# A hybrid decoder block on one core: bias rows made early and copied inside DRAM, one product for the norm row, wider products for the mixer's transposed blocks

## Chip, core and metric

One core of a Trainium2 chip runs the whole program in one launch. The metric is the device time of one execution in microseconds. The kernel before has a median of 1972.65 us over three runs (1972.31 to 1973.14).

## What is computed

One layer over `x` of 256 rows by 2048 columns, all in float32:

```python
x = x + 0.5 * swiglu(rmsnorm(x, ffn1_norm), ffn1_w1, ffn1_w3, ffn1_w2)     # 2048 -> 5632 -> 2048
x = x + token_mix(rmsnorm(x, mix_norm), w_in, ...)
x = x + 0.5 * swiglu(rmsnorm(x, ffn2_norm), ffn2_w1, ffn2_w3, ffn2_w2)
return rmsnorm(x, final_norm)
```

`token_mix` projects `x` with one matrix `w_in` to the queries and keys of four retention heads, their values and gates, and the queries, keys and values of an attention of eight heads in two groups with three branches (compressed blocks, selected blocks, a window). The compressed branch runs 32 rows at a time through a small network (`cw1k`, `cw2k` for keys, `cw1v`, `cw2v` for values). A table of 8 heads by 32 buckets gives each logit a bias that depends on the distance of query and key alone; it is added in all three branches.

## The kernel before

**Products in two parts.** Every large weight comes as float32 tiles of 128 partitions by 1024 columns (512 KB). Class `Weights` takes them in one fixed order (`specs`): `load` starts a transfer on SP's queue into one of four `raw` buffers, `divide` makes `hi` by a cast on ScalarE (L153) and `lo` by a subtraction on VectorE (L154), three buffers of each. `next` gives the tile that is due and keeps two further tiles divided. The activations are split in the same way, and a product is three: hi by hi, lo by hi, hi by lo.

**Work between tiles.** `W.later(n, fn)` has `fn` written into the program when the n-th tile from now is taken; a scheduler then sets the order on each engine, and may place what depends on nothing far earlier. Each engine and each queue works in its order.

**Stages.** `ffn` runs twice: 176 tiles for the two upward matrices, in which a tile is 8 products of 512 columns and 8 of 256 (`up_tile`, L418 and L420: the moving operand of the first holds both parts of `x` side by side), then 88 tiles for the downward one (`unit_b`, L387 to L389). Between them lies `mixer`, with 152 tiles. Its results that are wanted transposed come from `pair_a`: two column blocks of 256 at a time, eight tiles, 24 products of 256 columns each (L366, L368, L370) into one accumulator a block; the caller reads the accumulators. There are eight such pairs: compressed keys and values; selected and window keys; two for the queries, the first with the tiles of `cw1k` and `cw1v` in turn with its own (`compress`, L683 to L685); four for the retention heads (`retain`, with `rotate`, `decay`, `values` laid between the next tiles). `attend` is laid between the tiles after the queries.

**Norms.** `norm_start` sums squares and makes `rs`, the reciprocal root, on POOL (L323, L324). `norm_row` turns it into a row that all partitions hold: two products of ones by a diagonal (`n1d`, one buffer, L339 and L340).

**The bias.** At the mixer's start SP's queue gets nine small loads (L568): `pe`, `relb` (the table), `oh` (97 rows of 2 KB that pick the bucket for each distance), `cs`, `cw2k`, `cw2v`, `cmask`, `dec`, `gn`. `bias_table` splits the table in three, makes one row a head (`vrow`, 8 by 384) with a product (L586), and writes it 128 times to DRAM from eight partitions (L592, `scr`, 1536 KB); six tiles later one load with a step of one element less a row reads it back as diagonals (L594, `bias`, 1024 KB).

Of the kernel before, what the change touches and what calls it, by code (L numbers as in the profile page):

```python
# [7 lines left out]
F32 = mybir.dt.float32  # L8
# [178 lines left out]
def body(tc, nc, I, out, keep, wp, st, pp, dr):  # L187
# [12 lines left out]
    def add(name, idx, n=1024):  # L200
        specs.append((I[name][idx], n))
# [22 lines left out]
    for k in range(3):
        add("win_a", 20 + k)
        add("cw1v", k)
    add("win_a", 19)
    add("cw1k", 3)
    add("win_a", 23)
    add("cw1v", 3)  # L230
    add_pair("win_a", 6, "win_a", 7)
# [6 lines left out]
    for h in range(RH):  # L238
        add_pair("win_a", 8 + 2 * h, "win_a", 9 + 2 * h)
# [115 lines left out]
    def pair_a(x, after=None):  # L355

        pa, pb = pm("pa"), pm("pb")
        for acc, c in [(pa, 0), (pa, 1), (pa, 2), (pb, 0), (pb, 1), (pb, 2), (pa, 3), (pb, 3)]:
            hi, lo = W.next()
            hi = hi[:, :1024].rearrange("p (k n) -> p k n", k=4)  # L360
            lo = lo[:, :1024].rearrange("p (k n) -> p k n", k=4)
            for f in range(2):
                o = acc[:, f * S:(f + 1) * S]
                cs = slice(f * P, (f + 1) * P)
                for k in range(4):
                    nc.tensor.matmul(o, lo[:, k, cs], x[c][:, k, 0, :], start=(c == 0 and k == 0 and f == 0),  # L366
                                     stop=False, skip_group_check=True)
                    nc.tensor.matmul(o, hi[:, k, cs], x[c][:, k, 0, :], start=False, stop=False,  # L368
                                     skip_group_check=True)
                    nc.tensor.matmul(o, hi[:, k, cs], x[c][:, k, 1, :], start=False,  # L370
                                     stop=(c == 3 and k == 3), skip_group_check=True)
            if after:
                after()
        return pa.rearrange("p (f s) -> p f s", f=2), pb.rearrange("p (f s) -> p f s", f=2)
# [125 lines left out]

    x2, x3 = [], []
# [5 lines left out]
    with tc.tile_pool(name="mx", bufs=1) as mp:  # L507
        mixer(nc, I, keep, mp, st, dr, ps, W, ident, x2, rs[1], lambda: norm_row(rs[1], "n1"),
              pair_a, unit_b, lhs_x(x2), rsqrt, into(x3, ss3, 2, 1.0))
# [35 lines left out]
    ffn(x3, lambda: norm_row(rs[2], "n2"), 5, finish, True)  # L545


def mixer(nc, I, keep, mp, st, dr, ps, W, ident, x2, rs, get_row, pair_a, unit_b, lhs, rsqrt, finish):
# [11 lines left out]
    oh = mp.tile([97, 2, 512], BF16, tag="L1", name="oh", bufs=2)  # L560
# [3 lines left out]
    relb = mp.tile([96, 8], F32, name="relb")  # L564
    w2 = [mp.tile([P, P], F32, name=f"w2{n}") for n in "kv"]
    for j, (t, n) in enumerate(((pe, "pe"), (relb, "relb"), (oh, "oh"), (cs, "cs"), (w2[0], "cw2k"), (w2[1], "cw2v"),
                                (cmask, "cmask"), (dec, "dec"), (gn, "gn"))):
        later(2 + j, lambda t=t, n=n: nc.sync.dma_start(t, I[n]))  # L568
# [52 lines left out]
    pc = pair_a(x2)  # L621
# [3 lines left out]
    kv = mp.tile([P, 2, G, S], F32, tag="t4", name="kv", bufs=3)  # L625
# [3 lines left out]
    def blocks(b):  # L629
        tt(kv[:, b], pc[b], row(R, 2), ALU.mult)  # L630
# [44 lines left out]
    turns = [(0, 0), (0, 1), (0, 2), (1, 0), (1, 1), (1, 2), (0, 3), (1, 3)]  # L675
# [13 lines left out]
    for j in range(2):  # L689
        for k, p in enumerate(pair_a(x2, compress if j == 0 else None)):  # L690
            h = 4 * j + 2 * k
            nc.vector.scalar_tensor_tensor(nq[:, h:h + 2, :], p, SCALE, row(R, 2), op0=ALU.mult, op1=ALU.mult)
# [109 lines left out]
    def retain(h, pq, pk):  # L802
        qk = mp.tile([P, 2, 2, S], F32, tag="t4", name="qk", bufs=3)

        def rotate(i, p):
# [34 lines left out]
        rotate(0, pq)  # L840
        later(1, lambda: rotate(1, pk))
# [3 lines left out]
    for h in range(RH):  # L845
        retain(h, *pair_a(x2))
# [60 lines left out]
```

## Time and profile before

| | |
|---|---|
| median of the runs | 1972.65 us |
| the profiled execution | 1973.32 us, its span 1971.5 us |
| TensorE busy | 1935.5 us (98%), weight loads 1677.7 us |
| VectorE, ScalarE, POOL busy | 1153.1, 893.6, 9.9 us |
| moved by DMA | 365.45 MB, mean 185 GB/s |
| granted clock of TensorE, mean | 0.993 |

Times in the rows are from the span's start. Products overlap: a row's duration is longer than the step to the next one, so pace is read from starts. The granted clock is a share of 2.4 GHz. DMA issues are not part of an engine's busy time; the issues of SP stand as SPq.

### The profile page before, as it was taken

To read this page: it belongs to the slowest core of one execution; us is meant where nothing else is said; L and a number is where in the kernel's file an instruction comes from. 1 tells how busy PE (TensorE), PEld (TensorE's weight loads), DVE (VectorE), ACT (ScalarE), POOL (GpSimd) and SP (SyncE) were. 2 spreads that over 40 slices of the span, in tenths; PEclk is the share of its full clock that TensorE was granted. 3 is DMA by queue.
4 is the path that set the end of the run, shared out by engine and by line. 5 is a ranking of instruction groups with operands and counts; after the bars stand their busy time and mean duration, and the time that the engine had idled before them with its cause. 6 is when DMAs were issued, how large, how long until landed. Compare 5 with 4: busy or idle time off the path is not lost.

```text
span 1971.5 us, 27203 instructions
## 1 busy us (share of the span) xinstructions
PE 1935.5 (98%) x10753; PEld 1677.7 (85%) x10753; DVE 1153.1 (58%) x1488; ACT 893.6 (45%) x1268; POOL 9.9 (1%) x27
## 2 busy tenths in 40 slices
PE   8999999999999999699999999999999999999998
PEld 7888888888888889598999888888888888888886
DVE  6666666666554446255677555666666666644444
ACT  6444444444444344244444444444444444434343
POOL 0000000000000000000000000000000000000000
PEclk9999999999999999799999999999999999999999
DMA  7666666666666656665444455666666666666664
GB/s 274 192 187 191 187 190 190 188 187 192 187 187 183 190 183 197 158 219 173 148 146 135 169 182 182 182 190 187 190 191 185 190 192 186 210 190 185 191 185 146
DMA packets 103354, 365.45 MB, mean 185 GB/s; under 512 B 11865, under 2 KB 14425, under 8 KB 102842
## 3 DMA queue, kind: packets, MB, share of 16 engines
q1 hardware_dynamic: 102794, 363.43, 60.3%
q8 instruction: 84, 1.38, 0.3%
q10 hardware_dynamic: 432, 0.29, 0.1%
q14 instruction: 44, 0.36, 0.0%
HBM read 360.00 MB, written 3.67 MB: 184 GB/s over the span
## 4 chain that ended last, share of the span: by engine, by line
PE 96%; DMA 3%; ACT 0%; DVE 0%; issue 0%; ACTq 0%; POOLq 0%; POOL 0%
PE pu L418 16%; PE pv L418 16%; PE p L388 12%; PE p L387 12%; PE p L389 12%; PE pu L420 8%; PE pv L420 8%; DMA raw<-in_cw1k 2%; PE pa L366 1%; PE pa L368 1%; PE pa L370 1%; PE pb L366 1%; PE pb L368 1%; PE pb L370 1%; PE up L418 1%; PE o L774 1%
## 5 line engine op out<-in xcount | busy, mean ns | idle before, releaser
L154 DVE TENSOR_TENSOR lo<-raw,hi 128x1024 fp32r<-128x1024 f32 (+2 forms) x673 | 823.9, 1224 | 649.1 <-ACT hi L153 648.6
L153 ACT CAST hi<-raw 128x1024 fp32r<-128x1024 f32 (+2 forms) x673 | 704.3, 1047 | 788.9 <-PE p L389 382.2
L387 PE MATMUL p<-hi,hh 128*128 128x512 f32 x704 | 279.4, 397 | 0.0
L388 PE MATMUL p<-lo,hh 128*128 128x512 f32 x704 | 278.7, 396 | 0.0
L389 PE MATMUL p<-hi,hl 128*128 128x512 f32 x704 | 278.6, 396 | 0.0
L418 PE MATMUL pu<-x3c,hi 128*128 128x512 f32 x672 | 264.5, 394 | 0.0
L418 PE MATMUL pv<-x1c,hi 128*128 128x512 f32 x672 | 264.3, 393 | 0.0
L418 PE MATMUL pu<-x1c,hi 128*128 128x512 f32 x672 | 264.3, 393 | 0.0
L418 PE MATMUL pv<-x3c,hi 128*128 128x512 f32 x672 | 264.3, 393 | 0.0
L420 PE MATMUL pu<-x1c,lo 128*128 128x256 f32 x672 | 189.5, 282 | 0.0
L420 PE MATMUL pu<-x3c,lo 128*128 128x256 f32 x672 | 189.2, 282 | 0.0
L420 PE MATMUL pv<-x1c,lo 128*128 128x256 f32 x672 | 189.2, 282 | 0.0
L420 PE MATMUL pv<-x3c,lo 128*128 128x256 f32 x672 | 189.1, 281 | 0.0
L389 PEld LDWEIGHTS p<-hi,hl 128*128 128x128 f32 x704 | 132.1, 188 | 32.3
L387 PEld LDWEIGHTS p<-hi,hh 128*128 128x128 f32 x704 | 132.5, 188 | 31.7
L388 PEld LDWEIGHTS p<-lo,hh 128*128 128x128 f32 x704 | 132.4, 188 | 31.1
L418 PEld LDWEIGHTS pu<-x3c,hi 128*128 128x128 f32 x672 | 126.2, 188 | 28.7 <-DVE u L195 0.2
L418 PEld LDWEIGHTS pu<-x1c,hi 128*128 128x128 f32 x672 | 126.3, 188 | 28.4 <-DVE u L195 0.2
L418 PEld LDWEIGHTS pv<-x3c,hi 128*128 128x128 f32 x672 | 126.2, 188 | 28.4
L418 PEld LDWEIGHTS pv<-x1c,hi 128*128 128x128 f32 x672 | 126.3, 188 | 28.3
L420 PEld LDWEIGHTS pv<-x3c,lo 128*128 128x128 f32 x672 | 126.7, 189 | 0.0
L420 PEld LDWEIGHTS pu<-x3c,lo 128*128 128x128 f32 x672 | 126.5, 188 | 0.0
(225 smaller groups left out, 2444.3 us busy)
## 6 DMA issues: line engine op xcount, KB each, us to landing
raw<-in_ffn_w SPq DMA_DIRECT2D x527, 512.0 KB, 3.7
raw<-in_win_a SPq DMA_DIRECT2D x64, 512.0 KB, 3.9
raw<-in_win_b SPq DMA_DIRECT2D x32, 512.0 KB, 3.2
raw<-in_wout SPq DMA_DIRECT2D x32, 512.0 KB, 3.3
raw<-in_win_vg SPq DMA_DIRECT2D x4, 560.0 KB, 3.8
xs<-in_x SPq DMA_DIRECT2D x2, 1024.0 KB, 9.7
raw<-in_cw1k SPq DMA_DIRECT2D x4, 512.0 KB, 21.6
raw<-in_cw1v SPq DMA_DIRECT2D x4, 512.0 KB, 4.5
```

The lines of the kernel that those rows point to most:

```text
L153: self.nc.scalar.copy(hi[:, s], raw[:, s])
L154: self.nc.vector.tensor_tensor(lo[:, s], raw[:, s], hi[:, s].bitcast(F32), op=ALU.subtract)
L366: nc.tensor.matmul(o, lo[:, k, cs], x[c][:, k, 0, :], start=(c == 0 and k == 0 and f == 0), stop=False, skip_group_check=True)
L368: nc.tensor.matmul(o, hi[:, k, cs], x[c][:, k, 0, :], start=False, stop=False, skip_group_check=True)
L370: nc.tensor.matmul(o, hi[:, k, cs], x[c][:, k, 1, :], start=False, stop=(c == 3 and k == 3), skip_group_check=True)
L387: nc.tensor.matmul(acc[t][:, :width], a, hi[:, k, :], start=first, stop=False)
L388: nc.tensor.matmul(acc[t][:, :width], a, lo[:, k, :], start=False, stop=False)
L389: nc.tensor.matmul(acc[t][:, :width], b, hi[:, k, :], start=False, stop=last)
L418: nc.tensor.matmul(acc, hi[:, k, f, :], xk.rearrange("p j s -> p (j s)"), start=(kt == 0), stop=False, skip_group_check=True)
L420: nc.tensor.matmul(acc[:, :S], lo[:, k, f, :], xk[:, 0, :], start=False, stop=(kt == KT - 1), skip_group_check=True)
L774: nc.tensor.matmul(o[:, q0:], v, p, start=start, stop=stop, skip_group_check=True)
```

## The change

- `relb` and `oh` are loaded at tile 40 of the first FFN and `vrow` is made at tile 60, both as written, in tiles that live through the whole program; POOL issues the transfers. `vrow` goes to DRAM once (`scr1`), and at tile 80 one transfer copies it 128 times from DRAM to DRAM (`scr`).
- The seven remaining small loads and the load of `bias` are issued by POOL at the mixer's start, and not by SP.
- `norm_start` makes both diagonals, and `norm_row` is one product of 256 columns.
- A block's tile is as in `up_tile`: 8 products of 512 columns and 8 of 256, into two accumulators. `close_a` adds their halves: a copy on ScalarE and an addition on VectorE for each accumulator, into SBUF, from where the callers read. The first pair keeps its order of tiles; all others are single blocks of four tiles (`block_a`), and the list of tiles follows. In the queries' first two blocks the four tiles of `cw1k` go with the first, those of `cw1v` with the second.

```diff
@@ tiles @@
-    for k in range(3):
-        add("win_a", 16 + k)
-        add("cw1k", k)
...
+    for j, n in enumerate("kv"):
+        for t in range(4):
+            add("win_a", 16 + 4 * j + t)
+            add(f"cw1{n}", t)
...
@@ norm_start, norm_row @@
-        return rs
-
-    def norm_row(rs, name):
+        dg = st.tile([P, 2, P], F32, tag="xg", name=name + "d", bufs=3)
+        for t in range(2):
+            nc.vector.tensor_scalar(dg[:, t, :], ident, rs[:, t:t + 1], None, op0=ALU.mult)
+        return rs, dg
+
+    def norm_row(dg, name):
         pr = ps(name + "p")
-        for t in range(2):
-            dg = st.tile([P, P], F32, tag="dg", name=name + "d", bufs=1)
-            nc.vector.tensor_scalar(dg, ident, rs[:, t:t + 1], None, op0=ALU.mult)
-            nc.tensor.matmul(pr[:, t * P:(t + 1) * P], ones, dg, start=True, stop=True)
+        nc.tensor.matmul(pr[:, :S], ones, dg.rearrange("p t s -> p (t s)"), start=True, stop=True)
@@ blocks @@
+    def tile_a(x, accs, c):
+        hi, lo = (w[:, :1024].rearrange("p (k n) -> p k n", k=4) for w in W.next())
+        for k in range(4):
+            xk = x[c][:, k]
+            for f, acc in enumerate(accs):
+                cs = slice(f * P, (f + 1) * P)
+                nc.tensor.matmul(acc, hi[:, k, cs], xk.rearrange("p j s -> p (j s)"), start=(c == 0 and k == 0),
+                                 stop=False, skip_group_check=True)
+                nc.tensor.matmul(acc[:, :S], lo[:, k, cs], xk[:, 0, :], start=False, stop=(c == 3 and k == 3),
+                                 skip_group_check=True)
+
+    def close_a(accs, dst):
+        for f, acc in enumerate(accs):
+            nc.scalar.copy(dst[:, f, :], acc[:, S:])
+            tt(dst[:, f, :], acc[:, :S], dst[:, f, :], ALU.add)
+
+    def block_a(x, dst, after=None):
+        accs = pm("pa"), pm("pa")
+        for c in range(CH):
+            tile_a(x, accs, c)
+            if after:
+                after()
+        close_a(accs, dst)
...
@@ bias, ahead of the first FFN @@
+    def bias_rows():
...
+        nc.gpsimd.dma_start(scr1, vrow[:, :384])
+
+    def bias_loads():
+        nc.gpsimd.dma_start(relb, I["relb"])
+        nc.gpsimd.dma_start(oh, I["oh"])
+
+    W.later(40, bias_loads)
+    W.later(60, bias_rows)
+    W.later(80, lambda: nc.gpsimd.dma_start(scr, bass.AP(tensor=scr1.tensor, offset=scr1.offset,
+                                                         ap=[[0, P], [384, 8], [1, 384]])))
@@ mixer @@
-        later(2 + j, lambda t=t, n=n: nc.sync.dma_start(t, I[n]))
+    for t, n in ((pe, "pe"), (cs, "cs"), (w2[0], "cw2k"), (w2[1], "cw2v"), (cmask, "cmask"), (dec, "dec"), (gn, "gn")):
+        nc.gpsimd.dma_start(t, I[n])
...
+    diag = bass.AP(tensor=scr.tensor, offset=scr.offset + 127, ap=[[8 * 384 - 1, P], [384, 8], [1, S]])
+    nc.gpsimd.dma_start(bias[:, :, 16:], diag)
...
-        later(2, lambda: nc.sync.dma_start(scr.rearrange("q h r -> h q r"),
-                                           vrow[:, None, :].to_broadcast([8, P, 384])))
-        later(8, lambda: nc.sync.dma_start(bias[:, :, 16:], diag))
...
@@ retain @@
-        rotate(0, pq)
-        later(1, lambda: rotate(1, pk))
+        block_a(x2, qk[:, 0])
+        rotate(0)
+        block_a(x2, qk[:, 1])
+        later(1, lambda: rotate(1))
```

**POOL, from the program's start to the mixer's, before** (`masks.py` makes the identity, `n0s` and `n1s` are the norms' reciprocal roots, L614 to L616 clear tiles of the mixer):

```order
masks.py:197 MEMSET ident 128x128
masks.py:199 ISA
masks.py:199 AFFINE_SELECT ident<-ident 128x128 [waits Pool_49]
L323 TENSOR_SCALAR n0s<-n0t 128x2 [waits DVE_49]
L324 TENSOR_TENSOR n0s<-n0s,mhalf 128x2 [waits Pool_49]
L614 MEMSET vcmp 128x256 [waits DMAHW3_49,DMAHW4_49,DMAHW2_49,DMAHW5_49,DMAHW0_49,DMAHW6_49,DVE_49,PE_49]
L615 MEMSET ptc 128x512
L616 MEMSET kcat 128x2
L323 TENSOR_SCALAR n1s<-n1t 128x2 [waits DVE_49]
L324 TENSOR_TENSOR n1s<-n1s,mhalf 128x2 [waits Pool_49]
```

The same stretch of the change:

```order
L535 DMA relb<-in_relb 96x8
masks.py:199 ISA
masks.py:199 AFFINE_SELECT ident<-ident 128x128 [waits Pool_49]
L536 DMA oh<-in_oh 97x1024
L320 TENSOR_SCALAR n0s<-n0t 128x2 [waits DVE_49]
L321 TENSOR_TENSOR n0s<-n0s,mhalf 128x2 [waits Pool_49]
L532 DMA scr_99<-vrow 8x384 [waits DVE_49]
L540 DMA scr<-scr_99 128x3072 [waits DMASW2_49]
L607 DMA pe<-in_pe 128x64 [waits DMAHW3_49,DMAHW4_49,DMAHW2_49,DMAHW5_49,DMAHW0_49,DMAHW6_49,DVE_49,PE_49]
L607 DMA cs<-in_cs 128x512
L607 DMA w2k<-in_cw2k 128x128
L607 DMA w2v<-in_cw2v 128x128
L607 DMA cmask<-in_cmask 128x16 [waits DMASW0_49]
L320 TENSOR_SCALAR n1s<-n1t 128x2 [waits DVE_49]
L607 DMA dec<-in_dec 128x1024 [waits DMASW1_49]
L321 TENSOR_TENSOR n1s<-n1s,mhalf 128x2 [waits Pool_49]
```

`relb` and `oh` stand at the very start and wait for nothing; `scr_99` is `scr1`. Five of the mixer's loads now stand ahead of `n1s`, and a sixth between its two steps.

**VectorE at the program's start, before** (`lo` is a weight's subtraction, `x1c` the first FFN's activations):

```order
L286 MEMSET mhalf 128x16
L154 TENSOR_TENSOR lo<-raw,hi 128x512 [waits DMAHW1_49,Activation_49]
L283 SCALAR_TENSOR_TENSOR x1c_74<-landed,gains,x1c_74 128x256 [waits DMAHW4_49,DMAHW0_49,Activation_49]
L283 SCALAR_TENSOR_TENSOR x1c_74<-landed,gains,x1c_74 128x256 [waits DMAHW2_49,Activation_49]
L154 TENSOR_TENSOR lo<-raw,hi 128x512 [waits DMAHW3_49,Activation_49]
```

And with the change:

```order
L523 CAST part_1722<-relb 96x8 [waits DMASW0_49]
L524 COPY rb<-part_1722 32x8 [waits DVE_49]
L195 TENSOR_TENSOR relb<-relb,part_1722 96x8
L523 CAST part_1723<-relb 96x8 [waits DVE_49]
L524 COPY rb<-part_1723 32x8 [waits DVE_49]
L195 TENSOR_TENSOR relb<-relb,part_1723 96x8
L523 CAST part_1724<-relb 96x8 [waits DVE_49]
L524 COPY rb<-part_1724 32x8 [waits DVE_49]
L154 TENSOR_TENSOR lo<-raw,hi 128x512 [waits DMAHW1_49,Activation_49]
L280 SCALAR_TENSOR_TENSOR x1c_74<-landed,gains,x1c_74 128x256 [waits DMAHW4_49,DMAHW0_49,Activation_49]
```

The table's eight operations, the first of which waits for the load that POOL issues, now stand ahead of the first subtraction.

**VectorE at the mixer's start, with the change** (`n1t` is the sum of squares, `xg` and `x2c` the last transposed activations):

```order
L326 TENSOR_REDUCE n1t<-ss_101 128x2 [waits Activation_49]
L594 TENSOR_TENSOR blk<-pe,blk 128x16x2 [waits DMASW4_49,Activation_49]
L594 TENSOR_TENSOR blk<-pe,blk 128x16x2 [waits Activation_49]
L154 TENSOR_TENSOR lo<-raw,hi 128x1024 [waits DVE_49,DMAHW0_49,PE_49,Activation_49]
L331 TENSOR_SCALAR n1d<-ident,n1s 128x128 [waits Pool_49]
L331 TENSOR_SCALAR n1d<-ident,n1s 128x128
L256 TENSOR_TENSOR xg<-pt,gains 128x512 [waits PE_49]
L154 TENSOR_TENSOR lo<-raw,hi 128x1024 [waits DMAHW1_49,DVE_49,Activation_49]
L195 TENSOR_TENSOR x2c_6433<-xg,x2c_6433 128x4x128 [waits Activation_49]
```

Both halves of `n1d` stand together and ahead of the next subtraction; before, the second one stood four subtractions later. `blk<-pe` has moved ahead of a subtraction.

## Rows read from the trace of the kernel before

**Rows 1.** Waits of TensorE over the whole span: line, whose work it waited for, us in total, times, longest.

```profile
PE phk L683 <- ACT hi L153: 18.8, 1, 18.8
PE up L418 <- DVE x1c L283: 3.0, 1, 3.0
PE n1p L340 <- DVE n1d L339: 1.6, 1, 1.6
PE up L418 <- ACT hi L153: 1.4, 1, 1.4
PE phk L684 <- DVE lo L154: 0.8, 1, 0.8
```

**Rows 2.** TensorE in order of time around its longest wait: start, duration, line, operation, and in brackets the idle time before it and what ended it.

```profile
805.70 0.28 PE L370 MATMUL pa<-x2c,hi 128*128 128x256 f32 x1
824.76 0.43 PE L683 MATMUL phk<-hi,blk 128*34 128x256 f32 x1 [18.79 <-ACT hi L153]
...
830.72 0.28 PE L370 MATMUL pa<-x2c,hi 128*128 128x256 f32 x1
```

**Rows 3.** Stretches: length, busy us and instructions of TensorE, its weight loads, VectorE, ScalarE, POOL; then granted clock, mean busy share of the DMA engines, GB/s.

```profile
172.00:228.00 56.00, 56.00 (x323) 49.25 (x322) 35.78 (x46) 26.95 (x41) 0.00 (x0) 1.00 0.63 188
...
794.00:797.00 3.00, 3.00 (x27) 3.00 (x26) 1.28 (x2) 1.05 (x1) 0.00 (x0) 1.00 0.46 49
...
827.00:830.00 3.00, 3.00 (x16) 2.79 (x15) 1.75 (x3) 1.25 (x2) 0.00 (x0) 0.50 0.76 221
...
833.00:836.00 3.00, 3.00 (x28) 2.97 (x26) 2.28 (x2) 1.56 (x2) 0.00 (x0) 1.00 1.06 402
...
1000.00:1030.00 30.00, 30.00 (x236) 29.33 (x235) 23.39 (x56) 12.63 (x28) 0.88 (x2) 1.00 0.42 126
```

**Rows 4.** SP's queue in order of time: start, duration of the issues, line, transfer, count.

```profile
754.92 0.33 SPq L568 DMA_DIRECT2D oh<-in_oh  x1
...
766.29 0.33 SPq L568 DMA_DIRECT2D dec<-in_dec  x1
...
788.53 0.31 SPq L592 DMA_DIRECT2D scr<-vrow  x1
790.42 9.37 SPq L140 DMA_DIRECT2D raw<-in_cw1k  x1
```

**Rows 5.** The chain that ended last, in order of time: start, us, what.

```profile
755.43 12.11 DMA raw<-in_win_a
...
790.42 33.14 DMA raw<-in_cw1k
```

**Rows 6.** DMA issues by line: transfer, issuer, count, KB each, median us from issue to landing.

```profile
raw<-in_ffn_w SPq DMA_DIRECT2D x527, 512.0 KB, 3.7
...
bias<-scr SPq DMA_DIRECT2D x1, 1024.0 KB, 7.0
...
relb<-in_relb SPq DMA_DIRECT2D x1, 3.0 KB, 2.8
```

**Rows 7.** In order of time, columns as in rows 2: SP issuing the load into a raw buffer just freed (this row merges six loads, the first at its start), ScalarE casting that tile, then TensorE at the first and the last product of two tiles of a block, and at the same product of two tiles of the first FFN, six tiles apart.

```profile
738.62 14.33 SPq L140 DMA_DIRECT2D raw<-in_win_a  x6
...
747.49 1.05 ACT L153 CAST hi<-raw 128x1024 fp32r<-128x1024 f32 x1 [1.75 <-PE p L389]
...
752.89 0.28 PE L366 MATMUL pa<-x2c,lo 128*128 128x256 f32 x1
...
758.48 0.28 PE L370 MATMUL pa<-x2c,hi 128*128 128x256 f32 x1
...
199.91 0.39 PE L418 MATMUL pu<-x1c,hi 128*128 128x512 f32 x1
...
216.64 0.39 PE L418 MATMUL pu<-x1c,hi 128*128 128x512 f32 x1
```

**Rows 8.** Groups of instructions by shape, the FFN's closing of two accumulators: line, engine, operation, count, busy us, mean ns, idle time before.

```profile
L439 ACT COPY r<-pu 128x256 f32<-128x256 f32 x84 | 31.3, 372 | 122.3 <-PE pu L420 122.3
L195 DVE TENSOR_TENSOR u<-pv,r 128x256 f32<-128x256 f32 x84 | 35.1, 418 | 0.0
```

**Rows 9.** The program's start: one stretch with the columns of rows 3, then VectorE and ScalarE in order of time.

```profile
10.00:15.00 5.00, 5.00 (x26) 4.27 (x26) 4.73 (x8) 4.39 (x9) 0.00 (x0) 0.85 1.05 413
...
7.71 0.88 DVE L283 SCALAR_TENSOR_TENSOR x1c<-landed,gains,x1c 128x256 fp32r<-128x256 f32 x2 [2.23 <-ACT x1c L282]
...
19.40 0.63 ACT L319 ACTIVATE junk<-xs 128x512 f32<-128x512 f32 x1 [1.02 <-DMA xs<-in_x]
```

**Rows 10.** Waits of SP's queue over the whole span: whose work, us, times, longest.

```profile
SPq L568 <- DMA oh<-in_oh: 4.2, 1, 4.2
```

**Rows 11.** The mixer's start in order of time: SP, POOL, VectorE, ScalarE.

```profile
753.08 1.32 SPq L568 DMA_DIRECT2D pe<-in_pe  x1
...
756.08 0.70 POOL L324 TENSOR_TENSOR n1s<-n1s,mhalf 128x2 f32<-128x2 f32 x1
...
756.82 0.29 DVE L339 TENSOR_SCALAR n1d<-ident,n1s 128x128 f32<-128x128 f32 x1 [1.10 <-POOL n1s L324]
...
758.80 1.05 ACT L153 CAST hi<-raw 128x1024 fp32r<-128x1024 f32 x1 [1.36 <-PE pa L370]
...
759.92 0.69 DVE L259 TENSOR_TENSOR xg<-pt,gains 128x512 f32<-128x512 f32 x1
760.52 1.22 DVE L154 TENSOR_TENSOR lo<-raw,hi 128x1024 fp32r<-128x1024 f32 x1
```

More of the change, by code (lines that the diff above doesn't have):

```diff
@@ L218, in body @@
     add_pair("win_a", 0, "win_a", 1)
-    add_pair("win_a", 2, "win_a", 3)
-    for k in range(3):
-        add("win_a", 16 + k)
-        add("cw1k", k)
[L224 to L231, printed above, removed]
+    for t in range(8, 16):
+        add("win_a", t)
+    for j, n in enumerate("kv"):
+        for t in range(4):
+            add("win_a", 16 + 4 * j + t)
+            add(f"cw1{n}", t)
+    for t in range(24, 32):
+        add("win_a", t)
     for t in range(4):
@@ L238, in body @@
     for h in range(RH):
-        add_pair("win_a", 8 + 2 * h, "win_a", 9 + 2 * h)
+        for t in range(8):
+            add("win_a", 32 + 8 * h + t)
     for t in range(16, 32):
@@ L372, in pair_a @@
+    def close_a(accs, dst):
[6 more added lines that the diff above has]
+            tile_a(x, accs, c)
             if after:
                 after()
-        return pa.rearrange("p (f s) -> p f s", f=2), pb.rearrange("p (f s) -> p f s", f=2)
+        close_a(accs, dst)
+    def pair_a(x, da, db):
+        aa, ab = [(pm("pa"), pm("pa")) for _ in range(2)]
+        for accs, c in [(aa, 0), (aa, 1), (aa, 2), (ab, 0), (ab, 1), (ab, 2), (aa, 3), (ab, 3)]:
+            tile_a(x, accs, c)
+        close_a(aa, da)
+        close_a(ab, db)
@@ L499, in into @@
         return f
+    oh = keep.tile([97, 2, 512], BF16, name="oh")
+    relb = keep.tile([96, 8], F32, name="relb")
+    rb = keep.tile([97, 8], BF16, name="rb")
+    scr1 = dr.tile([8, 384], F32, name="scr1")
+    scr = dr.tile([P, 8, 384], F32, name="scr")
+    def bias_rows():
+        part = [keep.tile([96, 8], BF16, name=f"part{j}") for j in range(3)]
+        for j in range(3):
+            nc.vector.tensor_copy(part[j], relb)
+            nc.vector.tensor_copy(rb[32 * j:32 * j + 32, :], part[j][32 * j:32 * j + 32, :])
+            if j < 2:
+                tt(relb, relb, part[j], ALU.subtract)
+        nc.vector.memset(rb[96:97, :], 1.0)
+        vp = ps("vp")
+        nc.tensor.matmul(vp[:8, :], rb, oh[:, 1, :], start=True, stop=True)
+        vrow = st.tile([8, 512], F32, tag="junk", name="vrow", bufs=1)
+        nc.vector.tensor_copy(vrow[:, :384], vp[:8, :384])
+        nc.gpsimd.dma_start(scr1, vrow[:, :384])
[6 more added lines that the diff above has]
+                                                         ap=[[0, P], [384, 8], [1, 384]])))
     x2, x3 = [], []
@@ L507, in body @@
     with tc.tile_pool(name="mx", bufs=1) as mp:
-        mixer(nc, I, keep, mp, st, dr, ps, W, ident, x2, rs[1], lambda: norm_row(rs[1], "n1"),
-              pair_a, unit_b, lhs_x(x2), rsqrt, into(x3, ss3, 2, 1.0))
+        mixer(nc, I, keep, mp, st, scr, oh, rb, ps, W, ident, x2, rs[1][0], lambda: norm_row(rs[1][1], "n1"),
+              pair_a, block_a, unit_b, lhs_x(x2), rsqrt, into(x3, ss3, 2, 1.0))
     ss4 = st.tile([P, 2, CH + 1], F32, name="ss4")
@@ L543, in finish, with mixer @@
                 nc.sync.dma_start(out[t * P:(t + 1) * P, 512 * k:512 * k + 512], x)
-    ffn(x3, lambda: norm_row(rs[2], "n2"), 5, finish, True)
-def mixer(nc, I, keep, mp, st, dr, ps, W, ident, x2, rs, get_row, pair_a, unit_b, lhs, rsqrt, finish):
+    ffn(x3, lambda: norm_row(rs[2][1], "n2"), 5, finish, True)
+def mixer(nc, I, keep, mp, st, scr, oh, rb, ps, W, ident, x2, rs, get_row, pair_a, block_a, unit_b, lhs, rsqrt, finish):
     later = W.later
@@ L638, in mixer @@
     later(4, lambda: tt(cs, cs, row(R, 2), ALU.mult))
-    pks, pkw = pair_a(x2)
-    tt(kcat[:, :, 16:], pks, row(R, 2), ALU.mult)
-    tt(kw, pkw, row(R, 2), ALU.mult)
+    for dst in (kcat[:, :, 16:], kw):
+        block_a(x2, dst)
+        tt(dst, dst, row(R, 2), ALU.mult)
     hidT = [mp.tile([P, 30], F32, name=f"hidT{b}") for b in range(2)]
@@ L674, in mixer @@
     ph = [ps("phk"), ps("phv")]
-    turns = [(0, 0), (0, 1), (0, 2), (1, 0), (1, 1), (1, 2), (0, 3), (1, 3)]
+    turns = [(b, i) for b in range(2) for i in range(4)]
     def compress():
@@ L687, in compress @@
             compress_end(b, ph[b])
[L689 to L692, printed above, removed]
+    for j in range(4):
+        q = nq[:, 2 * j:2 * j + 2, :]
+        block_a(x2, q, compress if j < 2 else None)
+        nc.vector.scalar_tensor_tensor(q, q, SCALE, row(R, 2), op0=ALU.mult, op1=ALU.mult)
     for j, width in ((0, 280), (1, 256)):
```

49 lines of the change are left out of this document (8 added, 41 removed).

## The prediction

> **What bounds the kernel now.** I read the waits of TensorE first [rows 1]. They show the reader that TensorE stands still for some 26 us of 1971.5, and that one wait makes most of it: 18.8 us before the first product of `compress` (L683), for the cast of a weight tile on ScalarE. The sequence of TensorE around it [rows 2] shows where it lies and that it costs more than its idle time: the last product before it starts at 805.70, the next at 824.76, another pause of 0.8 us follows for the subtraction [rows 1], and products go on slowly until 830.72. The stretches [rows 3] show why: after the pause, in 827 to 830, TensorE is busy throughout but the granted clock is 0.50 (1.2 GHz); in 833 to 836 it is 1.00 (2.4 GHz), and 28 products start in 3 us instead of 16.
>
> What the cast waits for stands in the queue of SP and in the chain [rows 4, 5]: at 788.53 SP issues `scr<-vrow` (1.5 MB), right behind it the load of a `cw1k` tile, which takes 33.14 us to land where a weight tile usually takes 3.7 [rows 6]. In 794 to 797 the sixteen engines move 49 GB/s, though their mean busy share is 0.46 [rows 3]: few of them work, and slowly. The weights are queued behind them on the same queue. So the bound is TensorE everywhere but here, at the first products, and at `n1p` (1.6 us) [rows 1].
>
> **How much lateness the weights bear.** It decides most of what follows. At 738.62 a raw buffer is free and SP loads into it; the cast of that tile starts at 747.49, waiting for a product and not for the load, which at the usual 3.7 us landed at 742.3, 5.2 us early. Cast and subtraction (1.05 and 1.22 us, [rows 7, 11]) end at 749.8, and with three `hi` buffers the products start two tiles after the cast began, at 753.1: another 3.3 us [rows 6, 7]. A transfer may thus come some 8.5 us late before TensorE waits. The trace agrees: behind `oh` a weight tile took 12.11 us, 8.4 more than usual [rows 5], and no product waited for it.
>
> **The change, part by part.**
>
> *The broadcast write leaves the mixer.* SP's queue no longer holds `scr<-vrow`, `oh`, or the other small loads. Gone is the whole delay of [rows 2]: without it, the product after 805.70 starts at 805.82, and 23 products (12 of `phk`, 11 of `pa`) at 0.117 to 0.119 us bring TensorE to 808.53; in the trace the next one starts at 830.72. That is **22.2 us**, clock included. The last weights before this stage came in time, and the stage's demand (tiles of 2.8 and 1.4 us in turn, so 512 KB in 2.1 us, 250 GB/s) is below the 402 GB/s that the queue reached in 833 to 836 [rows 3].
>
> *The norm row.* In the trace the second `n1d` waits for the first product (one buffer) and so falls behind a late subtraction; TensorE waits 1.6 us [rows 1]. Now both halves are made at once by `norm_start`, long before the product: **1.6 us** gone. One 256-wide product in place of two 128-wide ones changes under 0.2 us at three places; I put nothing down.
>
> *The transposed blocks.* A tile is now 8 products of 512 columns and 8 of 256, in place of 24 of 256. The old form: 48 products from 752.89 to the one that would follow 758.48 (758.60), so 2.855 us a tile. The new form is that of the FFN's `up_tile`: six tiles from 199.91 to 216.64, 2.788 us a tile [rows 7]. Eight pairs of blocks are 64 tiles: 64 x 0.067 = **4.3 us**. The columns are the same; what shrinks is the number of weight loads, 24 to 16.
>
> The price is `close_a`: for each of 16 blocks two copies on ScalarE and two additions on VectorE, by the FFN's rows 0.37 and 0.42 us [rows 8], so 0.74 and 0.84 us a block, in 11 us and more of products. VectorE is busy 0.78 of the fullest stretch (1000 to 1030) [rows 3]; 1.7 us more for a pair makes it 0.84. I cost it at nothing. The tightest place is the first pair, which takes all four accumulators: the next block wants the second accumulator of the first one about 3.1 us after its last product, and one cast, one subtraction and both closes (1.05 + 1.23 + 0.8) stand before it. If that cover is gone it costs tenths of a us, once. Products read `qk` three tiles after its block ends, as before, with some 3 us more work ahead of them in 8.4 us.
>
> *The early loads.* The order shows that `relb` and `oh` are issued by POOL at the program's very start, not at tile 40, and that VectorE has the splitting of `relb` ahead of its first subtraction. Here the sixteen engines are full: 413 GB/s in 10 to 15 us [rows 9]. 197 KB more at that rate are 0.5 us, and they come out in full, since TensorE waits for casts behind `xs`, the last of these loads [rows 1, 9]. `relb` took 2.8 us on SP [rows 6]; issued at about 1 us, with 1.3 us for the eight small operations, it is done before the first `x1c` at 7.71. From below the cost is 0. From above it is the trace's own `oh`: issued at 754.92, and SP, which waited 4.2 us for its landing, goes on at 766.29 [rows 4, 10]: 11.4 us for 194 KB, what one engine of sixteen would need and not sixteen. I take **+0.5**, nearer to the lower end, since this queue is another one, and keep 11.4 for the range.
>
> *The copy inside DRAM*, 1.5 MB early in the first FFN, beside weights at 188 GB/s [rows 3] of 400 or so. On free engines it takes 1.5 MB / 210 GB/s = 7.5 us; at the pace of `scr<-vrow` itself, 33 us. With half of the engines' time the weights keep 200 GB/s, so nothing is lost in the first case; in the second they lose at most a quarter of their pace for 33 us, 8 us, about their slack. Nothing put down. The loads at the mixer's start, 2 MB with `bias<-scr` (which landed in 7.0 us beside weights [rows 6]), are covered in the same way.
>
> *POOL's queue.* `n1s` now stands behind five DMA issues, and a sixth between its two steps. VectorE has `n1d` in order behind it, and behind that the subtraction of a tile cast at 758.80, whose products start 5.9 us later, at 764.7. 0.6 + 0.7 + 1.2 us of VectorE lie between, so `n1s` may come at 762.2; before it was ready at 756.8 [rows 7, 11]. No row has a DMA issue of POOL. The unhindered ones of SP are 0.33 to 1.32 us [rows 4, 11]: six are 2 to 7.9 us from 753.1, and `n1s` at 756 to 762, just in time. I take **+0.5** for the wait on `pe` and on this, 0 and 5 as ends.
>
> The sum goes against the profiled execution, 1973.3 us (span 1971.5): 1973.3 - 22.2 - 1.6 - 4.3 + 0.5 + 0.5 = **1946.2 us**. The median of the runs, 1972.65, lies 0.7 lower, well inside the range.
>
> **Rivals.**
>
> *`oh` on one engine at the start.* For it: the 11.4 us of [rows 4, 10]. Against it: the new queue, of which no row tells. That engine would share its time between `oh` and its part of every first load; `xs` would land some 8 us later, and TensorE pays it: **1954 us** (1951 to 1957). The Trainium skill ("DMA: Bandwidth & Descriptors", section "Why a DMA increments its semaphore by 16 and not by 1") says that the number of engines is the largest divisor up to 16 of the slowest dimension, so 1 for 97 rows, and 8 for the 8 rows of `vrow`; by that rule the sum would be this rival's 1954 us. The trace agrees on the queue of SP. The same section says that some copies issued by POOL are spread by rows over up to 16 engines all the same, which no run here shows.
>
> *POOL too slow for `n1s`.* If an issue takes 2 us or more, `n1s` comes at 766 or later and VectorE's queue, the weights' subtractions in it, stands: 3 to 6 us, **1950 us**. The Trainium skill ("SBUF — State Buffer", section "SBUF: two separate sides") says that VectorE in some modes keeps POOL from writing descriptors, which would do this; no row here shows it.
>
> *The copy or the gather takes more of the weights' time than their slack.* The wait moves rather than goes: half of it back, **1957 to 1965 us**. For it: such transfers were slow here. Against it: the weights are no longer behind them in one queue.
>
> *Slower.* The copy of 1.5 MB runs on one engine in the first FFN. By the pace of `oh` it takes 92 us alone; an engine that the weights need for 0.63 of the time gives them half while it lasts, some 185 us, and every tile waits for its slowest part: 185 x (1 - 0.5/0.63) = 38 us, less 8.5 of slack. It decides from 28 + 8.5 us of lost weight time; with long pieces of the copy taking more than half, it is more: **1975 to 2000 us**. Against it: the copy has 128 rows, and `bias<-scr`, with as many, moved 1 MB in 7.0 us [rows 6].
>
> **How the numbers follow.** Forecast (1943 to 1949): 0.62. `oh` narrow: 0.14. POOL late: 0.13. Transfers over the slack: 0.06. Slower or back to nothing: 0.03. Better than 1943: 0.02. The range takes in the first three: 1941 to 1957. A measurement here tells about 0.2%, 4 us, from no change. Faster by more than that are all cases but the last rival and the tail of the fourth: 0.95; within it 0.02, slower 0.03.
>
> **What would show it.** Right: no wait of TensorE at the first `phk` product; granted clock 1.00 throughout 800 to 840; about 2.79 us a tile in the blocks; weights landing in some 4 us around `scr<-scr1`. Wrong: a longer first 30 us (`oh`), VectorE idle before `n1d` or before `blk<-pe` at the mixer's start (POOL), casts that wait for DMA during the copy or the gather, or waits of TensorE for the closes.

## The result and the profile after

The changed kernel takes **1948.33 us** (median of 4 runs, 1948.16 to 1949.17), beside 1972.89 for the kernel before in the same session: ratio 0.9873, 95% interval 0.9862 to 0.9885, so 24.6 us less. The forecast was 1946.2 in a range of 1941 to 1957. The time lies in the range, 2.1 us over the forecast. The profiled execution took 1949.17 us (span 1947.4), 0.84 over the median, against 1973.32 (1971.5) before: 24.15 us less.

TensorE's waits of 0.5 us and over, which answer to [rows 1] (columns as there):

```profile
PE up L429 <- DVE x1c L280: 4.1, 1, 4.1
PE up L429 <- ACT hi L153: 1.8, 1, 1.8
PE warm L286 <- DVE ones L282: 1.0, 1, 1.0
PE up L431 <- DVE lo L154: 0.5, 1, 0.5
```

The waits at `phk` and at `n1p` are gone. All that is left lies in the first 30 us, and there it has grown: 4.1 us where [rows 1] has 3.0.

Four stretches with the columns of [rows 3]: part of the start, the copy inside DRAM, the place of the old wait, the 30 us in which VectorE is fullest.

```profile
5.00:10.00 5.00, 0.87 (x5) 0.58 (x4) 2.64 (x11) 1.28 (x3) 0.00 (x0) 1.00 0.96 314
...
186.00:197.00 11.00, 11.00 (x65) 9.67 (x64) 6.49 (x9) 5.37 (x8) 0.54 (x1) 1.00 0.91 287
...
800.00:840.00 40.00, 40.00 (x264) 35.37 (x262) 26.87 (x33) 20.94 (x26) 0.00 (x0) 1.00 0.74 227
...
1030.00:1060.00 30.00, 30.00 (x173) 26.28 (x173) 24.98 (x54) 13.73 (x28) 0.88 (x2) 1.00 0.49 151
```

In 800 to 840 TensorE is busy throughout at a granted clock of 1.00; before, [rows 2, 3] had 19 us of idle time there and then 0.50. The copy takes place beside full work of TensorE. VectorE, with the closes, is busy 0.83 of its fullest 30 us; before, the fullest was 0.78 [rows 3], at an earlier time, since the mixer's work has moved.

The start in order of time, which answers to [rows 9]: POOL's two loads, then who waits for what.

```profile
1.28 0.73 POOL L535 DMA_DIRECT2D relb<-in_relb  x1 [0.36 <-issue]
2.37 0.60 POOL L536 DMA_DIRECT2D oh<-in_oh  x1
6.79 0.17 DVE L523 CAST part<-relb 96x8 bf16<-96x8 f32 x1 [5.68 <-DMA relb<-in_relb]
8.72 0.91 ACT L279 ACTIVATE x1c<-landed,gains 128x256 fp32r<-128x256 f32 x2 [3.93 <-DMA gains<-in_gains]
...
21.68 0.63 ACT L316 ACTIVATE junk<-xs 128x512 f32<-128x512 f32 x1 [1.39 <-DMA xs<-in_x]
```

And the issues, time to landing last, which answer to [rows 6]:

```profile
scr<-scr POOLq DMA_DIRECT2D x1, 1536.0 KB, 9.9
bias<-scr POOLq DMA_DIRECT2D x1, 1024.0 KB, 10.5
...
oh<-in_oh POOLq DMA_DIRECT2D x1, 194.0 KB, 7.6
...
gains<-in_gains ACTq DMA_DIRECT2D x1, 24.0 KB, 7.0
relb<-in_relb POOLq DMA_DIRECT2D x1, 3.0 KB, 5.5
```

`gains` (24 KB) lands 7.0 us after its issue; in the trace of before it was 5.4. The first `x1c` waits for it, and `xs` then comes 2.3 us later: `junk<-xs` starts at 21.68, in [rows 9] at 19.40. From 5 to 10 us the DMA engines move 314 GB/s, and 397 before, at nearly the same busy share (0.96 and 1.03). The trace of before, columns of [rows 3]:

```profile
5.00:10.00 5.00, 2.00 (x8) 1.61 (x7) 2.50 (x5) 2.83 (x6) 0.00 (x0) 0.81 1.03 397
```

The mixer's start, which answers to [rows 11]: POOL issues before and between the two steps of `n1s`.

```profile
756.55 0.58 POOL L607 DMA_DIRECT2D pe<-in_pe  x1 [569.40 <-DVE xs L499]
...
759.32 0.19 POOL L320 TENSOR_SCALAR n1s<-n1t 128x2 f32<-128x2 f32 x1
759.57 0.58 POOL L607 DMA_DIRECT2D dec<-in_dec  x1
...
760.17 0.74 POOL L321 TENSOR_TENSOR n1s<-n1s,mhalf 128x2 f32<-128x2 f32 x1
...
761.45 0.91 POOL L615 DMA_DIRECT2D bias<-scr  x1
```

An issue of POOL takes 0.53 to 0.91 us. `n1s` is ready at 760.91, some 4.8 us into the mixer, and no product waits for it.

**The time by stages.** The two traces, and those of the runs below, were cut at the starts of TensorE's products. "Start" ends at ScalarE's first copy `r<-up`; "up" are the FFN's products `up`, `pu`, `pv`, to the start of their last one; "down 1" ends at the mixer's first product, the mixer at the second FFN's first, "down 2" (the products `p`) at the start of its last; "end" is the rest of the span. All in us.

| kernel | start | up 1 | down 1 | mixer | up 2 | down 2 | end | span |
|---|---|---|---|---|---|---|---|---|
| before | 33.83 | 469.93 | 249.13 | 470.76 | 492.34 | 246.29 | 9.27 | 1971.55 |
| changed | 36.10 | 470.86 | 249.14 | 442.30 | 492.85 | 246.28 | 9.84 | 1947.36 |
| e1 both loads late | 34.08 | 470.85 | 249.14 | 442.30 | 492.84 | 246.28 | 9.82 | 1945.30 |
| e2 `oh` late | 34.49 | 470.85 | 249.14 | 442.29 | 492.84 | 246.28 | 9.83 | 1945.73 |
| e3 `relb` late | 34.83 | 470.84 | 249.14 | 442.29 | 492.85 | 246.28 | 9.80 | 1946.04 |
| e4 three products | 35.27 | 470.86 | 249.14 | 446.58 | 492.85 | 246.28 | 9.83 | 1950.82 |
| e5 changed, again | 36.35 | 470.85 | 249.14 | 442.29 | 492.85 | 246.28 | 9.82 | 1947.58 |
| e6 before, POOL's queue | 33.53 | 469.92 | 249.12 | 466.62 | 492.40 | 246.29 | 9.22 | 1967.12 |
| e7 before, copy in DRAM | 34.08 | 469.96 | 249.12 | 448.45 | 492.35 | 246.29 | 9.34 | 1949.59 |
| e8 row in two | 35.96 | 471.00 | 249.14 | 442.38 | 492.93 | 246.28 | 9.84 | 1947.52 |
| e11 late, padded | 33.90 | 473.73 | 249.12 | 442.66 | 495.78 | 246.27 | 9.83 | 1951.28 |
| e12 late, other place | 33.98 | 470.34 | 246.41 | 442.40 | 492.38 | 243.57 | 9.82 | 1938.89 |

The mixer gained 28.46 us. Given back were 2.27 at the start, 0.93 and 0.51 in the two "up" stages, 0.57 at the end.

### The profile page after: what moved, and what is told of

Its sections match the earlier page's. It is cut to its first block, busy times and chain, and to the rows that moved or that the text cites. A ratio compares the mean times of both kernels' runs of the same rounds, so it can differ in the third digit from the quotient of the medians.

```text
span 1947.4 us, 26243 instructions
## 1 busy us (share of the span) xinstructions
PE 1930.4 (99%) x10235; PEld 1648.3 (85%) x10235; DVE 1164.6 (60%) x1520; ACT 901.7 (46%) x1300; POOL 17.2 (1%) x39
## 4 chain that ended last, share of the span: by engine, by line
PE 98%; DMA 1%; ACT 0%; DVE 0%; ACTq 0%; issue 0%; POOLq 0%; POOL 0%
PE pu L429 16%; PE pv L429 16%; PE p L399 12%; PE p L398 12%; PE p L400 12%; PE pv L431 8%; PE pu L431 8%; PE pa L359 6%; PE pa L361 3%; PE up L429 1%; PE o L797 1%; PE up L431 1%; DMA landed<-in_xt 1%; DMA xs<-in_x 0%; PE pt L347 0%; PE s L750 0%
## 5 line engine op out<-in xcount | busy, mean ns | idle before, releaser
L359 PE MATMUL pa<-x2c,hi 128*128 128x512 f32 x512 | 182.9, 398 | 0.0
L361 PE MATMUL pa<-x2c,lo 128*128 128x256 f32 x512 | 143.5, 280 | 0.0
```

The source lines that it names most:

```text
L359: nc.tensor.matmul(acc, hi[:, k, cs], xk.rearrange("p j s -> p (j s)"), start=(c == 0 and k == 0), stop=False, skip_group_check=True)
L361: nc.tensor.matmul(acc[:, :S], lo[:, k, cs], xk[:, 0, :], start=False, stop=(c == 3 and k == 3), skip_group_check=True)
```

## The experiments

Each is told as the difference of its median to that of the kernel before in the same session (1973.36 to 1973.75 us; the changed kernel: -24.6 us).

**e1, e2, e3: what the early loads cost.** Added ahead of the two loads, so that they must wait for tile 40 (POOL then issues `relb` at 122.22 in e1); in e3 the issue of `oh` also goes ahead of `relb`'s:

```diff
+        hi = W.parts[W.at][0].bitcast(F32)
+        nc.vector.tensor_copy(relb[:, 0:2], hi[:96, 0:2])      # e1, e3
+        nc.vector.tensor_copy(oh[:, 0, 0:2], hi[:97, 0:2])     # e1, e2
```

> The changed kernel, but relb and oh each get one small VectorE write from tile 40's weights first, so that their loads cannot start before about 100 us. Theory: the changed kernel's start is about 2.25 us longer (its first gate copy at 36.10 us against 33.83 us before) because these two loads run beside the first weights; then the start returns to 33.8 us and the time to 1946.1 us (1945.6 to 1946.6). Rival: the start is longer for another reason (other code, other semaphores of the SP queue's loads, the day's run), and the time stays at 1948.3 us with the first gate copy at 36 us.

> The changed kernel with oh alone held to tile 40; relb (3 KB) still loads at 1.3 us. If oh's 194 KB are what makes the gains and the first x slices land late (gains 7.0 us after issue against 5.4 us before): 1946.1 us, first gate copy at 33.8 us. If the VectorE's wait for relb ahead of its first weight split is the cause: 1948.3 us, and the split still begins at about 8 us. If both share it: 1947 us.

> The changed kernel with relb alone held to tile 40; oh is issued first on POOL's queue, at about 1.3 us. If oh's bytes are the cause: 1948.3 us or a little over (oh is issued 1.1 us earlier), VectorE's first split back at 4.8 us and TensorE's first product nevertheless at 9.5 us or later. If the wait for relb is the cause: 1946.1 us and the first product at 8.3 us.

Measured: 1946.99 (-26.8), 1947.18 (-26.6) and 1947.78 (-26.0) us. With both held the first gate copy is at 34.08 and `gains` lands in 5.5 us; in e2 it takes 6.2, in e3 6.6. The theory holds for the start; e1's 1946.99 lies over its range, but the kernel before took 0.9 us more beside it (1973.75) than beside the first runs, and the difference of 26.8 is the expected one. Neither load is the cause alone: the first gate copy is 0.4 us later than in e1 with `relb` early, 0.75 with `oh` early, about 2 with both. VectorE's wait is not what delays the first product: in e3 its first split is back at 4.93 and the first product is at 9.41 all the same, since `x1c` waits for `gains`. Why transfers of 3 and 194 KB make `gains` land later is not shown.

**e5: the changed kernel again**, beside e6 to e8.

> The changed kernel as it is, on the chip of the next three. If the 2.27 us by which its first profile's start was longer than before are what the early loads always cost: first gate copy at 36.1 us. If that execution's start was a long one, as the three-product kernel with the same loads (35.27 us) has it: about 35.3 us and 1948.2 us, so that the early loads cost 1.2 to 1.4 us.

Measured: 1948.91 us (-24.6), first gate copy at 36.35. The early loads cost 2.2 us by the runs (e1 against this). The start is as long as in the first profile, but made up otherwise: `gains` lands in 6.2 us, as in e2, and the first product starts at 8.98. Then, after five us with 2.77 of work, the granted clock is 0.66 in the mean of 25 to 30 us, a part of them at 0.50 (1.2 GHz). 21 products start there, in e2 (second fence) 31:

```profile
20.00:25.00 5.00, 2.77 (x14) 1.86 (x14) 1.23 (x1) 4.60 (x11) 0.00 (x0) 1.00 0.93 371
25.00:30.00 5.00, 5.00 (x21) 4.33 (x21) 3.28 (x6) 4.02 (x9) 0.92 (x2) 0.66 0.75 224
```

```profile
25.00:30.00 5.00, 5.00 (x31) 4.34 (x30) 3.38 (x6) 3.78 (x9) 0.91 (x2) 1.00 0.75 248
```

**e4: the blocks by three products.**

```diff
-                nc.tensor.matmul(acc, hi[:, k, cs], xk.rearrange("p j s -> p (j s)"), ...)
-                nc.tensor.matmul(acc[:, :S], lo[:, k, cs], xk[:, 0, :], ...)
+                for w, j in ((lo, 0), (hi, 0), (hi, 1)):
+                    nc.tensor.matmul(acc[:, :S], w[:, k, cs], x[c][:, k, j, :], ...)
...
-            nc.scalar.copy(dst[:, f, :], acc[:, S:])
-            tt(dst[:, f, :], acc[:, :S], dst[:, f, :], ALU.add)
+            nc.vector.tensor_copy(dst[:, f, :], acc[:, :S])
```

> The changed kernel with its 64 transposed-block tiles of the mixer computed as before, by three 256-wide products a step, closed by one VectorE copy from PSUM. Theory: a tile takes 2.855 us where the 512-wide and the 256-wide product take 2.788 us, so 64 x 0.067 = 4.3 us more: 1952.6 us (1952.0 to 1953.2). Rival: the gain of the blocks is smaller because the weights' arrival or the closes set the pace there: 1948.3 to 1950.5 us. Second rival: the closes' two operations (372 and 418 ns) were a cost that the old form lacks: under 1952 us by as much as they cost.

Measured: 1952.47 us (-21.3). The mixer takes 446.58 us, 4.28 more than the 442.30 of the changed kernel: the term of 4.3 to the decimal, and no cost of the closes is seen. The run as a whole is only 3.3 us longer than e5, since e4's start is 0.8 to 1.1 us shorter than the changed kernel's with the same two loads (35.27 against 36.10 and 36.35); why is open.

**e6, e7: the kernel before with its write alone changed.** e6 puts it on another queue, e7 gives it the other form on the same queue:

```diff
-        later(2, lambda: nc.sync.dma_start(scr.rearrange("q h r -> h q r"), vrow[...].to_broadcast([8, P, 384])))
-        later(8, lambda: nc.sync.dma_start(bias[:, :, 16:], diag))
+        later(2, lambda: nc.gpsimd.dma_start(scr.rearrange("q h r -> h q r"), vrow[...].to_broadcast([8, P, 384])))   # e6
+        later(8, lambda: nc.gpsimd.dma_start(bias[:, :, 16:], diag))                                                 # e6
+        later(2, lambda: nc.sync.dma_start(scr1, vrow))                                                              # e7
+        later(3, lambda: nc.sync.dma_start(scr, AP(scr1, [[0, P], [384, 8], [1, 384]])))                             # e7
```

> The kernel before with one thing changed: the broadcast write scr<-vrow and the gather bias<-scr are issued on POOL's queue instead of SP's, at the same places of the mixer. Theory: the weights waited because they stood behind the write in SP's queue; the 18.8 us wait and the half clock after it go, -22.2 us: 1951.5 us if the kernel before takes 1973.7. Rival: the write's few slow engines are what holds the weights, whatever queue it is on; then a good part of the wait stays, 1956 to 1974 us, and weights still land 15 us or more after issue while the write lasts.

> The kernel before with the broadcast write replaced, at the same place and on SP's queue: the 8 rows go to DRAM once (12 KB), and are copied 128-fold inside DRAM (1.5 MB) one tile later, ahead of the same weights. Theory that the transfer's shape (8 rows, 49 GB/s) was the cost: the copy takes about 10 us as it does in the changed kernel, weights behind it come 6 to 8 us late, within the 8.5 us they can bear: 1951.5 to 1954 us. Rival, that any 1.5 MB ahead of the weights in one queue stalls them, with SP held for two landings more: a wait of 5 to 15 us stays at the first phk product, 1957 to 1970 us.

Measured: e6 1968.61 us (-4.9), e7 1951.25 us (-22.2). TensorE's waits in e6 and the issues of its 785 to 830 us:

```profile
PE phk L683 <- ACT hi L153: 8.4, 1, 8.4
PE pa L366 <- DVE lo L154: 4.5, 1, 4.5
```

```profile
scr<-vrow POOLq DMA_DIRECT2D x1, 1536.0 KB, 35.8
raw<-in_cw1k SPq DMA_DIRECT2D x3, 512.0 KB, 22.8
```

The queue alone was not the cause: with the write on POOL's queue and SP's free, weights still take 22.8 us to land while it lasts. POOL's queue also cut the write otherwise, into 336 pieces of 4608 B and 8 of 3072 B, by the trace's records of single pieces; it took 33.0 us, on SP's queue 31.7. In e7 the 1.5 MB stand in SP's queue ahead of the same weights and the wait at `phk` is gone:

```profile
PE up L418 <- DVE x1c L283: 3.6, 1, 3.6
PE n1p L340 <- DVE n1d L339: 1.5, 1, 1.5
```

SP's queue in e7: the copy is issued at 791.05; SP issues the gather, which must wait for it, at 800.54.

```profile
790.57 0.33 SPq L140 DMA_DIRECT2D raw<-in_cw1k  x1
791.05 0.58 SPq L594 DMA_DIRECT2D scr<-scr  x1
...
800.54 0.46 SPq L596 DMA_DIRECT2D bias<-scr  x1
```

**e9, e10: which part of the form.** e9 copies inside DRAM by the old loops (8 rows outermost, 128 pieces of 1536 B each); e10 keeps the new loops but keeps the 1536 B pieces apart (rows padded to 400 numbers).

```diff
-        later(3, lambda: nc.sync.dma_start(scr, AP(scr1, [[0, P], [384, 8], [1, 384]])))
+        later(3, lambda: nc.sync.dma_start(scr.rearrange("q h r -> h q r"), AP(scr1, [[384, 8], [0, P], [1, 384]])))   # e9
+        later(3, lambda: nc.sync.dma_start(scr[:, :, :384], AP(scr1, [[0, P], [384, 8], [1, 384]])))                   # e10
```

> The kernel before with the 12 KB put into DRAM first and copied 128-fold there, as in the run with -22.2 us, but with the copy's loops in the order of the old broadcast write: 8 rows outermost, 128 pieces of 1536 B each. Theory: the old write was slow because its outermost size of 8 leaves it half of the engines, wherever the data come from; then this copy too takes 30 us or more to land, the wait of 15 to 19 us at phk is back and the time is 1968 to 1974 us. Rival: it was slow because each row was read 128 times from one SBUF partition; then the copy lands in about 10 us and the time is 1951 us.

> The same copy inside DRAM with its 1024 pieces of 1536 B kept apart (each row of scr padded to 400 numbers so that they do not merge), and an outermost size of 1024 instead of 8. If the outermost size decides: lands in 9 to 13 us, no wait at phk, 1951 us (1950 to 1953). If pieces of 1536 B instead of 12 KB made the old write slow: 25 us or more to land and 1962 to 1974 us. A middle result, 15 to 20 us and 1953 to 1960 us, would say that both count.

Measured: 1951.18 (-22.2) and 1951.32 us (-22.0). My theory of the eight rows fell; its rival, the source, holds. The stretch 794 to 797 of e9, which answers to the one in [rows 3]:

```profile
794.00:797.00 3.00, 3.00 (x28) 3.00 (x27) 1.23 (x1) 1.19 (x2) 0.00 (x0) 1.00 0.80 249
```

249 GB/s where the old write left 49. The records of single pieces tell why. One of 1536 B took 222 ns in the mean when read from `vrow` in SBUF (1024 pieces, 790.2 to 822.0); the same 1024 pieces took 66 ns read from DRAM in e9 (last end 801.4), 85 ns in e10. Mostly seven or eight pieces were under way at once in the old write, and still only eight or nine in e9: not their number but the time of each made the difference.

SBUF as a source is not slow by itself. The 8 pieces of 1536 B that e9 reads once out of the same `vrow` took 65 to 107 ns, and the 1024 pieces of 2048 B of `out_y`, read out of 128 rows of SBUF at the end of the kernel before, without weights beside them, 87 ns in the mean. What is left is that eight rows are read 128 times over. They gave 6.9 B a ns and piece, 50 GB/s in all, and in e6 with three times longer pieces 6.7 and 48; `out_y`'s pieces have 24 B a ns. That fits a limit on what eight rows of SBUF give together, but no run changes the number of rows.

**e8: the norm row in two products.**

```diff
+        for t in range(2):
+            dg = st.tile([P, P], F32, tag="dg", name=name + "d", bufs=1)
+            nc.vector.tensor_scalar(dg, ident, rs[:, t:t + 1], None, op0=ALU.mult)
+            nc.tensor.matmul(pr[:, t * P:(t + 1) * P], ones, dg, start=True, stop=True)
```

> The changed kernel with the norm row as before: two 128-wide products, the second diagonal made after the first product has read the one buffer. Theory: TensorE waits 1.6 us at n1p again, 1949.8 us against 1948.2. Rival: with POOL's n1s at 760.9 the first diagonal is late enough that more than 1.6 us is lost (1951), or the product falls where VectorE is free and nothing is lost (1948.2).

Measured: 1948.73 us (-24.7; e5 -24.6), mixer 442.38 against 442.29, and no wait at `n1p`. The old form costs 0.1 us here. The wait of before had another origin, by the trace of before, right ahead of it on ScalarE:

```profile
767.92 1.05 ACT L153 CAST hi<-raw 128x1024 fp32r<-128x1024 f32 x1 [4.07 <-DMA raw<-in_win_a]
```

This cast waited for the weight tile of [rows 5] that took 12.11 us behind `oh`; the subtraction followed late and the second `n1d` stood behind it. In e8 `oh` is loaded early, and the cast is in time. The other small loads have left SP's queue too in e8, so that `oh` is the one that the trace names, not one that was tried alone.

**e11, e12: why the "up" stages got longer.** The changed kernel, e1 to e5 and e8 take 22.34 us for four gate copies, where before, e6 and e7 take 22.31. e1 was run with unused space ahead of the weights, and with the added tiles behind them:

```diff
+    pad = keep.tile([P, 488], F32, name="pad")                    # e11
-    oh = keep.tile([97, 2, 512], BF16, name="oh")                 # e12; relb, rb, part likewise
+    oh = st.tile([97, 2, 512], BF16, name="oh", bufs=1)           # e12
```

> The changed kernel with oh and relb held to tile 40 (1947.0 us), and 1952 B a partition of unused space beside oh, relb and rb, so that what the change adds ahead of the weights' tiles in SBUF comes to 4096 B and not 2144. It is to settle why every variant of the change runs the FFNs' products 0.12% slower (22.34 us instead of 22.31 for four gate copies, 1.0 us in both FFNs) than the kernel before and its two variants. If the tiles' place in SBUF does it: the pace of before returns and 1946.0 us. If not: 1947.0 us, the pace as in the changed kernel.

> The changed kernel with oh and relb held to tile 40, and with oh, relb, rb and the three parts in the pool that lies behind the weights' pool, so that the weights' tiles lie in SBUF where they lay in the kernel before (without it: 1947.0 us; with 1952 B of unused space ahead of the weights: 1953.2 us). If the place of the weights' tiles sets the 0.12%: four gate copies take 22.31 us again and the time is 1946.0 us. If it is the place of other tiles (those of the FFN or the mixer, which lie behind this pool and still move): the pace stays at 22.34 us or takes a third value, 1947 us or more.

Measured: e11 1953.20 us (-20.2), e12 **1940.74 us** (-32.7; ratio 0.9837, interval 0.9824 to 0.9851), the fastest of all, below the changed kernel's interval. The same two gate copies, 52 copies apart, in the changed kernel, in e11 and in e12:

```profile
205.37 0.37 ACT L450 COPY r<-pu 128x256 f32<-128x256 f32 x1 [1.45 <-PE pu L431]
...
495.78 0.37 ACT L450 COPY r<-pu 128x256 f32<-128x256 f32 x1 [1.47 <-PE pu L431]
```

```profile
204.23 0.38 ACT L450 COPY r<-pu 128x256 f32<-128x256 f32 x1 [1.50 <-PE pu L431]
...
496.34 0.37 ACT L450 COPY r<-pu 128x256 f32<-128x256 f32 x1 [1.49 <-PE pu L431]
```

```profile
203.09 0.37 ACT L450 COPY r<-pu 128x256 f32<-128x256 f32 x1 [1.45 <-PE pu L431]
...
493.15 0.37 ACT L450 COPY r<-pu 128x256 f32<-128x256 f32 x1 [1.46 <-PE pu L431]
```

That is 290.41, 292.11 and 290.06 us, the last one before's own pace (202.53 to 492.59). Nothing waits: TensorE is busy throughout. So the place of tiles in SBUF changes the pace by up to 0.7%. My first theory holds for the "up" stages. What I did not expect is "down": 246.41 and 243.57 us in e12, 2.7 less in each FFN than in all other kernels, though its order of products is that of e1. More of them start in the same 100 us, in e12 (first fence) than in the changed kernel (second):

```profile
550.00:650.00 100.00, 100.00 (x444) 81.50 (x443) 51.50 (x48) 41.87 (x47) 0.00 (x0) 1.00 0.61 189
```

```profile
550.00:650.00 100.00, 100.00 (x438) 80.62 (x437) 50.27 (x47) 42.10 (x48) 0.00 (x0) 1.00 0.59 185
```

Which tiles' places matter there, and by what rule, stays open.

## Why the prediction was right, and where it was not

1. **The broadcast write, -22.2.** Right in size: in e7, which takes away nothing but this write's form, the mixer is 22.3 us shorter. Only half right in the reason: I saw that few engines worked, and slowly, but put the weights' delay to their place behind the write in SP's queue. In e6 another queue is worth 4.9 us; the rest goes with the slow pieces out of eight SBUF rows (222 ns each in the kernel before), on engines that the weights, by their 22.8 us in e6, also need. A change that had moved the write to POOL's queue as it was would have been forecast 17 us too fast by my reasoning.
2. **The norm row, -1.6.** The 1.6 us are gone, but not by the one product: e8 has the two and no wait. By the trace they belong to `oh`'s leaving SP's queue. My sentence that behind `oh` a tile came 8.4 us late "and no product waited for it" was wrong: `n1p` did, by way of VectorE. So 8.5 us is the slack of the weights' own chain, not of work that stands behind it on VectorE.
3. **The blocks, -4.3.** 4.28 in e4. The closes cost nothing that can be seen: VectorE's busy share is 0.83 at its fullest, where I had 0.84, and TensorE does not wait. My reason, fewer weight loads, was not tried on its own: e4 changes them together with the products' width and the closes.
4. **The early loads, +0.5: the step that failed.** They cost 2.2 us (e1 against e5). I counted bytes at 413 GB/s. What counts is that small transfers beside the first loads make those land later: `gains` by 1.6 us in the first profile, and what waits for it in turn (`x1c`, `xs`, the casts behind `junk`). In e5 it is 0.8 us, and the granted clock of 0.66 in 25 to 30 us adds to it; so the 2.2 us are shown by the runs, and their way is read from traces in which it is not always the same. The rival with one engine (1954 us) fell: `oh` took 7.6 us at the start and 3.7 in e1, with up to 13 of its pieces under way at once. The Trainium skill ("DMA: Bandwidth & Descriptors", section "Why a DMA increments its semaphore by 16 and not by 1") gave one engine for 97 rows, with an exception for some copies of POOL; here the exception held.
5. **POOL's queue, +0.5.** Nothing: before's 470.76 less 22.31 (e7), 4.28 (e4), 1.5 (the `n1p` wait) and 0.5 (the product `vp`, now in the first "up") is 442.2; measured 442.3. The rival fell: an issue took at most 0.91 us, `n1s` came at 760.9.
6. **The copy in DRAM, 0.** Right: 9.9 us to land, 287 GB/s in all, no wait. The rivals that rest on it fell.
7. **Not in the sum.** 0.9 us in the two "up" stages by the place of tiles (0.42 and 0.51, `vp` set aside), and 0.57 us at the end, where SP waits for some eight more semaphores, those of POOL's transfers; that last cause is read from the trace and was not tried.

Between the profiled executions: forecast -27.1, measured -24.15. Of the 2.95 us between, the start makes 1.8, the place of tiles 0.9, the end 0.6; the mixer gives back 0.35.

## What to carry to other kernels

When weights land late, compare how long one piece of the transfer beside them takes with a piece of theirs, before blaming the queue; here a small table that must be repeated 128 times was better copied from DRAM than broadcast out of eight SBUF rows. A load that is not needed early should be tied to work that comes late, since a queue with nothing else to do issues it into the fullest moment of the program. And when products that nothing changed run 0.1 to 1% slower or faster, look at where their tiles lie in SBUF: here that was worth more (6 us from e1 to e12) than two of the change's three parts.

## What the runs showed of the hardware

- One piece of 1536 B took 222 ns while eight SBUF rows were read 128 times over, 65 to 107 ns when the same rows were read once (e9), and 66 to 85 ns read from DRAM; 1.5 MB so took 31.7 us out of SBUF, and from DRAM beside weights 11.5 us with 8 rows outermost (e9) or 10.1 with 1024 pieces (e10).
- Weights on SP's queue took 22.8 us while such a write ran on POOL's: another queue alone does not keep transfers apart.
- 1952 B a partition of unused SBUF space made products with no wait 0.6% slower (292.11 against 290.4 us); another place of 2.1 KB of small tiles made the FFNs' last products 1.1% faster (246.41 against 249.14 us).
- POOL issued a transfer in 0.53 to 0.91 us beside a busy VectorE.
